# Mixer A of a two-layer encoder trunk: the left and right key tiles folded into one block before the softmax and put apart by GpSimd behind the transposes

## The chip, the cores and the metric

One core of one Trainium2 chip runs the whole program. The metric is the device time of one execution in microseconds (us), the median of three runs. Engine names as in the profile: PE is TensorE (matmuls and transposes), PEld its weight loads, DVE is VectorE, ACT is ScalarE, POOL is GpSimd, SP is SyncE, which mainly issues DMAs.

## The reference

Two layers over 1024 tokens (a grid of 16 rows by 64 columns) of width 1024 in fp32. Layer 0 uses mixer A, layer 1 mixer B; each is followed by a gated per-layer embedding, and one RMSNorm ends the trunk. Only mixer A is changed, and in it what the softmax of 16 heads of 64 works on:

```python
def mixer_a(h, w_in, rpb, w_out):
    proj = h @ w_in
    q, k, v, gate = jnp.split(proj, 4, axis=-1)          # 16 heads of 64
    ...                                                  # each query: a window of 8 rows x 16 columns of keys
    sc = jnp.einsum('bhqd,bhqnd->bhqn', qb, kg).astype(jnp.float32) * scale
    sc = sc + bb.astype(jnp.float32)[None]               # learned bias per offset
    pr = jax.nn.softmax(sc, axis=-1)
    o  = jnp.einsum('bhqn,bhqnd->bhqd', pr, vg)
    return (o * jax.nn.silu(gate)) @ w_out
```

A query at column c attends to the 16 columns from c - 8 on (clamped at the grid's edges).

## The kernel before, in words

Tokens are laid out in 8 tiles of 128: tile j holds the 8 grid columns 8j to 8j+7 of all 16 rows, so place p of a tile is row p // 8 and column p % 8 within the tile. With a window of 16 columns, the queries of tile j need keys of tiles j-1, j and j+1 alone: all of tile j, of tile j-1 the places whose column within the tile is at least the query's, and of tile j+1 those whose column is less. The mask `MK` says so with 1e30 in every other place, so for a query and a place of a tile, either the key in the left tile or the one in the right tile can count, never both.

Every fp32 product is made of fp32r pieces (a high part and the low rest), which is why most things exist twice: `PTh` and `PTl`, `HTh` and `HTl`, `wh` and `wl`. A head's q and k (transposed, 64 rows) are stacked to 128 rows: `QS` holds the high part of q in the lower 64 partitions and the low part in the upper, `KA` holds the high part of k twice, `KB` the low part of k twice.

**The attention steps.** `mixer_a` walks 128 steps (h, j): 16 heads of 8 query tiles. Step n issues, in this order, each as one item of a list:

- `f_T(n)`: transposes of the probabilities of step n by PE into the PSUM tile `t` (L723; two buffers), one for each key tile, so three for the inner tiles j = 1 to 6 and two for j = 0 and 7; ACT copies them as `PTh` (L726) and DVE subtracts the rest as `PTl` (L727). Both have 24 slots of 128 x 128: slot 3k + (j - k + 1) belongs to key tile k and query tile j, so that the up to three query tiles of one key tile lie side by side
- `f_E(n + 1)`: exponential on ACT over 384 columns (256 at j = 0 and 7), with the sum of each row (L715)
- `f_S(n + 2)`: scores of two steps ahead by PE into the PSUM tile `s` (two buffers), and on DVE, in one instruction, scores plus table `tb` and the minimum of each row, `mn` (L706; scores are negated, so that a minimum is the maximum)
- `f_AV(n - 2)`: PE multiplies v of key tile n - 2 with its slots of `PTh` and `PTl` into the PSUM tile `o`; it needs `f_T` up to step n - 1

**What runs beside.** `mix` puts pieces of dense work (the q/k projection of the next head, the gate, at the end p's projection) between the items, by a count of costs, and calls `pulse()` after each item of the steps: it loads and splits one weight tile when one is due (ACT `wh` L226, DVE `wl` L231), and counts down the list `post` of things to do a given number of pulses later. Among these are the splits of q and k, the evacuation of a head's output, and the tails of pairs of heads.

`qk_evac` copies q and k out of PSUM (ACT `th`, L647), and makes at pulses 2, 5 and 8 (`QD`): high q and high k on ACT (L650, L651); low q, low k and the second copy of high k on DVE (L654, L655, L656); the second copy of low k on DVE (L659).

`head_end` closes a head's half (four query tiles). For each pair of heads and half, two products follow on POOL, `Y*G` and `Y*rb` (L531, L532), where `rb` holds the reciprocal row sums and comes back from DRAM by DMA; they are issued at the head of a step, four steps after the half's last `f_AV`. Eleven pulses later ACT and DVE split Y (`rb<-Y` L528, L529). POOL also makes a head's table in five instructions (L681), and issues the DMAs that add up weights in DRAM (L597), one for each step in some heads.

Nothing is reordered at run time: each engine takes its instructions in the order in which the code issues them, and waits by semaphores.

Of the kernel before, what the change touches and what calls it, by code (L numbers as in the profile page):

```python
# [11 lines left out]
F32 = mybir.dt.float32  # L12
F32R = mybir.dt.float32r
# [28 lines left out]
THIRDS = {0: ((0, 1, 2), (0, 2, 1)), 1: ((0, 1, 2), (0, 1, 2))}  # L42
DP = 1
KD, KS = 3, 4
QD = (2, 5, 8)
QS_AT = 5
QO = (4, 6)
AGE, LAG = 3, 3
# [39 lines left out]
def lay_out(inp):  # L88
    g = {k: np.asarray(v) for k, v in inp.items()}
    W = np.empty((len(UNIT), 128, 1024), np.float32)  # L90

    def put(keys, cols, per):
        blk = cols.reshape(cols.shape[0] // 128, 128, -1).transpose(1, 0, 2)
        for u, key in enumerate(keys):
            W[UNIT[key]] = blk[:, u * per:(u + 1) * per].reshape(128, -1)

    aq, ak, av, ag = np.split(g["a_w_in"][0], 4, axis=1)
    for h in range(16):
        s = slice(h * HD, (h + 1) * HD)
        put([("aqk", h)], np.concatenate([aq[:, s], ak[:, s]], axis=1), 8)  # L100
    for q in range(4):
        put([("av", q, 0), ("av", q, 1)], av[:, q * 256:(q + 1) * 256], 4)
    bw = g["b_w_in"][0]
    bq, bk, bv, bg = bw[:, :1024], bw[:, 1024:1280], bw[:, 1280:1536], bw[:, 1536:]
    for p in range(8):
        s = slice(p * 128, (p + 1) * 128)
        put([("ag", p)], ag[:, s], 8)
        put([("bg", p)], bg[:, s], 8)
    for i in range(4):
        put([("bq", i, 0), ("bq", i, 1)], bq[:, i * 256:(i + 1) * 256], 4)  # L110
    for i in range(2):
# [24 lines left out]
    mask = np.where(ok, 0.0, BIG).astype(np.float32)  # L136

    inv = np.power(np.float32(10000.0), -np.arange(16, dtype=np.float32) * np.float32(2.0) / np.float32(32.0)).astype(np.float32)
    row = r.astype(np.float32)[:, None, None] + np.zeros((1, 8, 1), np.float32)
    col = (8 * np.arange(8)[None, :] + c[:, None]).astype(np.float32)[:, :, None]  # L140
    ar = (row * inv).astype(np.float32)
    ac = (col * inv).astype(np.float32)
    cosT = np.concatenate([np.cos(ar), np.cos(ar), np.cos(ac), np.cos(ac)], axis=2).astype(np.float32)
    sinT = np.concatenate([-np.sin(ar), np.sin(ar), -np.sin(ac), np.sin(ac)], axis=2).astype(np.float32)

    def swap(v):
        return v.reshape(2, 2, 16)[:, ::-1].reshape(64)

    bqn, bkn = g["b_q_norm"][0], g["b_k_norm"][0]
    hg = np.stack([bqn, swap(bqn), bkn, swap(bkn)])  # L150
    return {
        "x": tokens(g["x"][0]), "wts": W, "rpb": rpb, "gains": gains, "hgains": hg,
        "mask": mask, "rope": np.stack([cosT, sinT], axis=1),
        "gain0": gains[0].reshape(8, 128).T,
    }


@with_exitstack
def trunk(ctx, tc, x, wts, rpb, gains, hgains, mask, rope, gain0, out):
    nc = tc.nc  # L160
    sync, act, dve, pool, pe = nc.sync, nc.scalar, nc.vector, nc.gpsimd, nc.tensor

# [444 lines left out]
    def mixer_a():  # L607
        jobs = weight_sums()
        with ExitStack() as es:
# [4 lines left out]
            sb = es.enter_context(tc.tile_pool(name="asb", bufs=2))  # L614
            V = one.tile([128, NT, 4, 128], F32R, name="V")
            MK = one.tile([128, 5, 128], F32, name="MK")

            def dalloc():
                return pd.tile([128, 512], F32, name="d")
# [17 lines left out]
            def qk_evac(h, hf):  # L637
                def evac(ps):
                    if hf == 0:
                        QS[h] = qkp.tile([128, 1024], F32R, name="QS")  # L640
                        KA[h] = qkp.tile([128, 1024], F32R, name="KA")
                        KB[h] = qkp.tile([128, 1024], F32R, name="KB")
                    s = slice(hf * 512, (hf + 1) * 512)
                    lo, hi = slice(0, 64), slice(64, 128)
                    qs, ka, kb = QS[h], KA[h], KB[h]
                    raw = sb.tile([128, 512], F32, name="th", bufs=2)
                    act.activation(raw, ps, AF.Copy)  # L647

                    def one():
                        act.activation(qs[lo, s], raw[lo], AF.Copy, scale=-0.125)  # L650
                        act.activation(ka[hi, s], raw[hi], AF.Copy)  # L651

                    def two():
                        dve.scalar_tensor_tensor(qs[hi, s], raw[lo], -0.125, qs[lo, s], op0=ALU.mult, op1=ALU.subtract)  # L654
                        dve.tensor_tensor(kb[hi, s], raw[hi], ka[hi, s], ALU.subtract)  # L655
                        dve.tensor_copy(ka[lo, s], ka[hi, s])  # L656

                    def three():
                        dve.tensor_copy(kb[lo, s], kb[hi, s])  # L659
                    for i, f in enumerate((one, two, three)):  # L660
                        if h == 0:
                            f()
                        else:
                            post.add(QD[i], f)
                return evac

            def qk_items(h):
# [18 lines left out]
            def near(j):  # L686
                return max(j - 1, 0), min(j + 1, NT - 1)

            def f_S(h, j):
# [12 lines left out]
                else:  # L702
# [4 lines left out]
                                         in0=ps[:, :n].rearrange("p (k c) -> p k c", c=128), in1=tb,  # L707
                                         scale=1.0, scalar=1e38, op0=ALU.add, op1=ALU.min, accum_out=mn)
                SP[h, j] = (sp, mn)

            def f_E(h, j):
                k0, k1 = near(j)
                n = (k1 - k0 + 1) * 128
                sp, mn = SP[h, j]
                act.activation(sp[:, :n], sp[:, :n], AF.Exp, bias=mn, scale=-1.0, accum_out=RS[h][:, j:j + 1])  # L715

            def f_T(h, j):
                k0, k1 = near(j)
                m = k1 - k0 + 1
                sp, _ = SP.pop((h, j))  # L720
                ps = psT.tile([128, 4, 128], F32, name="t")
                for i in range(m):
                    pe.transpose(ps[:, i], sp[:, i * 128:(i + 1) * 128], ident)  # L723
                f0 = k0 * 3 + (j - k0 + 1)
                sl = slice(f0, f0 + 2 * m - 1, 2)
                act.activation(PTh[:, sl], ps[:, :m], AF.Copy)  # L726
                dve.tensor_tensor(PTl[:, sl], ps[:, :m], PTh[:, sl], ALU.subtract)  # L727

            def talloc():
                return psT.tile([128, 4, 128], F32, name="t")  # L730
# [122 lines left out]
            vs[1][1]()  # L853
            newton(4)
            sync.dma_start(MK, mask)
            for c in range(8):
                sync.dma_start(U[:, c], rpb[:, :, 7 - c:31 - c])
            for t in range(2, NT):
# [24 lines left out]
            psO = es.enter_context(tc.tile_pool(name="apo", bufs=2, space=PSUM))  # L883
            qkp = es.enter_context(tc.tile_pool(name="qkp", bufs=2))
            ptp = es.enter_context(tc.tile_pool(name="ptp", bufs=1))
            PTh = ptp.tile([128, NT * 3, 128], F32R, name="PTh")
            PTl = ptp.tile([128, NT * 3, 128], F32R, name="PTl")
            for d in qk_items(0):
                d[0]()
                WQ.pump()  # L890
# [12 lines left out]
            def av_and_v(h, kb):  # L903
                fs = [(lambda: f_AV(h, kb), CA[4])]
                if h % 4 == 3 and h < NH - 1:
                    fs += [(f, 0.0) for f in v_items(h // 4 + 1, kb)]
                return fs

            for h in range(NH):
                att = []  # L910
                for j in range(NT):
# [12 lines left out]
                        att.append((lambda n=n: f_E(*steps[n + 1]), CA[2]))  # L924
                    if n + 2 < len(steps):
                        att.append((lambda n=n: f_S(*steps[n + 2]), CA[3]))
                    if n >= 2:
                        att += av_and_v(*steps[n - 2])
                    if h == 15 and j >= YLOAD_A:
                        for t in ((j - YLOAD_A,) if j < NT - 1 else range(j - YLOAD_A, NT)):  # L930
                            att.append((lambda t=t: load_y(0, t), 0.0))
                    if h == 14 and j == OPEN3:
                        att.append((open3, 0.0))
                if h == NH - 1:
                    att += [(lambda: f_AV(NH - 1, NT - 2), CA[4]), (lambda: f_AV(NH - 1, NT - 1), CA[4])]
                dense = []
                if h < NH - 1:
                    dense += qk_items(h + 1)
# [754 lines left out]
    dense_phase(1)  # L1693


NAMES = ["x", "wts", "rpb", "gains", "hgains", "mask", "rope", "gain0"]


# [13 lines left out]
```

## Time and profile before

| what | value |
|---|---|
| median of three runs | 1531.36 us (1530.58 to 1531.82) |
| profiled execution, its own time | 1530.75 us |
| its span (first to last instruction) | 1529.0 us |
| PE, PEld busy | 1499.0 us (98%), 1312.1 us (86%) |
| DVE, ACT, POOL busy | 1099.1 us (72%), 899.6 us (59%), 305.0 us (20%) |
| mean granted TensorE clock | 0.999 |
| attention of mixer A | from about 60 us to about 522 us of the span |

The attention steps begin with the first transposes of probabilities at 60 us and end with the last ones at 522 us; a head takes about 24.5 us, and every fourth head about 42 us, since v of the next four heads is projected there. Matmuls overlap in the array, so PE counts as busy nearly throughout; what a matmul costs is read from the distance of starts, and what PE waits for from the idle time noted in a group's row. Durations of POOL are rough.

### The profile page before, as it was taken

How to read it: one execution, taken by the hardware profiler on the slowest of the kernel's cores; microseconds unless marked ns; L12 is line 12 of the kernel's file. 1: busy time of each engine (PE TensorE's matmuls, PEld its weight loads, DVE VectorE, ACT ScalarE, POOL GpSimd, SP SyncE). 2: the span in 40 equal slices, each digit the busy share in tenths (PEclk: the TensorE clock that was granted, in tenths of full speed). 3: DMA queues.
4: the chain of work that ended last, by engine and by line, in shares of the span. 5: the costliest groups of instructions: out<-in, count | busy, mean ns of one | idle time of the engine just before them, and what ended most of it. 6: DMA issues, size and time to landing. Idle time of an engine off the chain costs nothing.

```text
span 1529.0 us, 24364 instructions
## 1 busy us (share of the span) xinstructions
PE 1499.0 (98%) x8976; PEld 1312.1 (86%) x8976; DVE 1099.1 (72%) x2091; ACT 899.6 (59%) x1801; POOL 305.0 (20%) x413
## 2 busy tenths in 40 slices
PE   9999999999999999999999999999999999999997
PEld 8888988988988887888988889989899888778786
DVE  7666576477477499767877786777877777689856
ACT  6565465466366635433567776666767777744432
POOL 1222232242112000010312132443131300000022
PEclk9999999999999999999999999999999999999999
DMA  8325355262122863262210111111111122663123
GB/s 261 129 85 135 83 142 162 63 169 80 36 87 73 327 247 97 90 203 79 75 49 22 32 40 49 46 32 51 49 32 43 45 69 81 226 224 114 67 88 134
DMA packets 91096, 157.22 MB, mean 103 GB/s; under 512 B 18144, under 2 KB 54112, under 8 KB 90464
## 3 DMA queue, kind: packets, MB, share of 16 engines
q1 hardware_dynamic: 85824, 139.66, 27.4%
q0 software_dynamic: 2560, 8.39, 3.1%
q10 hardware_dynamic: 2592, 7.61, 1.4%
q8 instruction: 71, 1.16, 0.3%
q14 instruction: 49, 0.40, 0.1%
HBM read 125.10 MB, written 50.83 MB: 115 GB/s over the span
## 4 chain that ended last, share of the span: by engine, by line
PE 36%; DVE 10%; ACT 4%; issue 3%; DMA 0%; SPq 0%; ACTq 0%; DVEq 0%
PE d L317 17%; PE o L317 7%; PE t L1178 5%; PE s L317 5%; DVE PTl L1181 2%; DVE mn L1162 1%; ACT P L1168 1%; ACT PTh L1180 1%; PE t L317 1%; DVE xn L1498 1%; DVE QS L1142 0%; DVE wl L231 0%; DVE X L1394 0%; PE t L1132 0%; ACT wh L226 0%
## 5 line engine op out<-in xcount | busy, mean ns | idle before, releaser
L317 PE MATMUL d<-wh,HTh 128*128 128x256 f32 (+1 forms) x1032 | 343.0, 334 | 3.6 <-ACT HTh L446 0.8
L317 PE MATMUL d<-wh,HTl 128*128 128x256 f32 (+1 forms) x1032 | 337.9, 329 | 0.3 <-DVE HTl L447 0.3
L317 PE MATMUL d<-wl,HTh 128*128 128x256 f32 (+1 forms) x1032 | 337.2, 329 | 0.0
L1181 DVE TENSOR_TENSOR PTl<-t,PTh 128x512 fp32r<-128x512 f32 x256 | 164.4, 684 | 111.6 <-ACT PTh L1180 111.2
L317 PEld LDWEIGHTS d<-wh,HTh 128*128 128x128 f32 x1032 | 194.6, 189 | 24.3 <-ACT HTh L446 1.2
L317 PEld LDWEIGHTS d<-wl,HTh 128*128 128x128 f32 x1032 | 194.8, 190 | 18.9
L317 PEld LDWEIGHTS d<-wh,HTl 128*128 128x128 f32 x1032 | 194.7, 190 | 18.7 <-DVE HTl L447 0.5
L317 PE MATMUL d<-HTh,wh 128*128 128x512 f32 x504 | 206.0, 409 | 0.0
L317 PE MATMUL d<-HTh,wl 128*128 128x512 f32 x504 | 198.4, 394 | 0.0
L317 PE MATMUL d<-HTl,wh 128*128 128x512 f32 x504 | 197.6, 392 | 0.0
L1168 ACT ACTIVATE P<-s,mn 128x1024 f32<-128x1024 f32 x128 | 142.7, 1115 | 59.7 <-DVE mn L1162 59.0
L1180 ACT ACTIVATE PTh<-t 128x512 fp32r<-128x512 f32 x256 | 140.0, 593 | 44.6 <-PE t L1178 44.3
L1162 DVE TENSOR_REDUCE mn<-s 128x1 f32<-128x1024 f32 x128 | 154.8, 1210 | 12.3 <-PE s L317 12.2
L1178 PE MATMUL t<-ident,P 128*128 128x128 f32 x1024 | 137.6, 275 | 6.1 <-DVE PTl L1181 4.0
L317 PE MATMUL s<-KA,QS 128*128 128x512 f32 (+2 forms) x384 | 133.8, 402 | 0.0
L1178 PEld LDWEIGHTS t<-ident,P 128*128 128x128 f32 x1024 | 114.6, 140 | 21.9 <-DVE PTl L1181 15.9
L231 DVE TENSOR_TENSOR wl<-wstage,wh 128x1024 fp32r<-128x1024 f32 x78 | 101.0, 1300 | 35.6 <-ACT wh L226 35.1
L317 PE MATMUL s<-KB,QS 128*128 128x512 f32 (+2 forms) x384 | 121.8, 371 | 0.0
L727 DVE TENSOR_TENSOR PTl<-t,PTh 128x384 fp32r<-128x384 f32 (+1 forms) x128 | 66.6, 521 | 74.5 <-ACT PTh L726 73.3
L317 PE MATMUL o<-PTh,V 128*128 128x256 f32 (+2 forms) x672 | 118.9, 288 | 1.2 <-DVE Y L461 0.9
L317 PE MATMUL o<-PTl,V 128*128 128x256 f32 (+2 forms) x672 | 119.1, 288 | 0.1
L317 PEld LDWEIGHTS d<-HTh,wl 128*128 128x128 f32 x504 | 94.7, 188 | 21.5
(237 smaller groups left out, 2698.5 us busy)
## 6 DMA issues: line engine op xcount, KB each, us to landing
wstage<-in_wts SPq DMA_DIRECT2D x88, 512.0 KB
pp<-ppD SPq DMA_DIRECT2D x32, 256.0 KB
X<-in_x SPq DMA_DIRECT2D x15, 512.0 KB
rb<-rD SPq DMA_DIRECT2D x56, 128.0 KB
ppD<-th SPq DMA_DIRECT2D x20, 256.0 KB
tD0t<-in_wts SPq DMA_DIRECT2D x16, 256.0 KB
tD1t<-in_wts SPq DMA_DIRECT2D x16, 256.0 KB
xD<-X SPq DMA_DIRECT2D x8, 512.0 KB
```

The costliest lines, as they stand in the source:

```text
L231: eng.tensor_tensor(lo[:, c:c + n], s[:, c:c + n], hi[:, c:c + n], ALU.subtract)
L317: pe.matmul(ps, a, b, start=first, stop=last, skip_group_check=True)
L727: dve.tensor_tensor(PTl[:, sl], ps[:, :m], PTh[:, sl], ALU.subtract)
L1162: dve.tensor_reduce(mn, ps, axis=AX.X, op=ALU.min)
L1168: act.activation(p, ps, AF.Exp, bias=mn, scale=-1.0, accum_out=RS[h, hf][:, t:t + 1])
L1178: pe.transpose(ps[:, i], p[:, k * 128:(k + 1) * 128], ident)
L1180: act.activation(PTh[:, ks, c], ps, AF.Copy)
L1181: dve.tensor_tensor(PTl[:, ks, c], ps, PTh[:, ks, c], ALU.subtract)
L1498: dve.scalar_tensor_tensor(xn, X[t], rn[m][:, i:i + 1], g1, op0=ALU.mult, op1=ALU.mult)
```

## The change

The score instruction still covers three tiles and its row minimum. Then, for inner query tiles, a second DVE instruction writes the minimum of the left and the right block over the left one (128 x 128). The exponential covers 256 columns instead of 384, and two blocks are transposed instead of three. The middle one goes to its slot; the folded one goes to one of two new slots behind the 24 (by j's parity), and POOL multiplies it with the two 0/1 patterns of `SIDE` (key column not less than the query's; less) into the two slots of the left and the right key tile, once for `PTh` and once for `PTl`. `f_AV` runs three steps behind instead of two. `SIDE` is loaded once, behind `MK`. Apart from that, the second copies of high and low k move from DVE to ACT, and the five parts of the q/k split come at pulses 2, 4, 6, 7 and 9.

```diff
-QD = (2, 5, 8)
+QD = (2, 4, 6, 7, 9)
...
+    sides = np.stack([c[:, None] >= c[None, :], c[:, None] < c[None, :]], axis=1).astype(np.float32)
...
-                    def two():
+                    def low_q():
                         dve.scalar_tensor_tensor(qs[hi, s], raw[lo], -0.125, qs[lo, s], op0=ALU.mult, op1=ALU.subtract)
+
+                    def low_k():
                         dve.tensor_tensor(kb[hi, s], raw[hi], ka[hi, s], ALU.subtract)
-                        dve.tensor_copy(ka[lo, s], ka[hi, s])
-
-                    def three():
-                        dve.tensor_copy(kb[lo, s], kb[hi, s])
-                    for i, f in enumerate((one, two, three)):
+
+                    def across(k):
+                        act.activation(k[lo, s], k[hi, s], AF.Copy)
+                    parts = (one, low_q, lambda: across(ka), low_k, lambda: across(kb))
+                    for at, f in zip(QD, parts):
...
                 SP[h, j] = (sp, mn)
+                if 0 < j < NT - 1:
+                    dve.tensor_tensor(sp[:, 0:128], sp[:, 0:128], sp[:, 256:384], ALU.min)
 
             def f_E(h, j):
-                k0, k1 = near(j)
-                n = (k1 - k0 + 1) * 128
+                n = 256
...
             def f_T(h, j):
...
+                inner = 0 < j < NT - 1
+                for i in range(2):
+                    c = 1 - i if inner else i
+                    pe.transpose(ps[:, i], sp[:, c * 128:(c + 1) * 128], ident)
+                k0 = near(j)[0]
+                f0 = 3 * j + 1 if inner else k0 * 3 + (j - k0 + 1)
+                f1 = 3 * NT + j % 2 if inner else f0 + 2
+                sl = slice(f0, f1 + 1, f1 - f0)
+                act.activation(PTh[:, sl], ps[:, :2], AF.Copy)
+                dve.tensor_tensor(PTl[:, sl], ps[:, :2], PTh[:, sl], ALU.subtract)
+                if inner:
+                    def apart():
+                        for pt in (PTh, PTl):
+                            pool.tensor_tensor(pt[:, 3 * j - 1:3 * j + 4:4], pt[:, f1:f1 + 1].to_broadcast([128, 2, 128]), SIDE,
+                                               ALU.mult)
+                    apart()
...
+            sync.dma_start(SIDE, sides)
...
-            PTh = ptp.tile([128, NT * 3, 128], F32R, name="PTh")
-            PTl = ptp.tile([128, NT * 3, 128], F32R, name="PTl")
+            PTh = ptp.tile([128, NT * 3 + 2, 128], F32R, name="PTh")
+            PTl = ptp.tile([128, NT * 3 + 2, 128], F32R, name="PTl")
...
-                    if n >= 2:
-                        att += av_and_v(*steps[n - 2])
+                    if n >= 3:
+                        att += av_and_v(*steps[n - 3])
```

PE, in a head with no work on v, from one inner step's transposes to the next product with v, before (`t` the transposes, `d` dense work, `s` the scores, `o` the product with v):

```order
L723 MATMUL t<-ident,sp 128x128 x3
L317 MATMUL d<-HTh,wh_2073 128x512
L317 MATMUL d<-HTl,wh_2073 128x512
L317 MATMUL d<-HTh,wl_2074 128x512
L317 MATMUL d<-HTh,wh_2073 128x512
L317 MATMUL d<-HTl,wh_2073 128x512
L317 MATMUL d<-HTh,wl_2074 128x512
L317 MATMUL s<-KA,QS 128x384
L317 MATMUL s<-KB,QS 128x384
L317 MATMUL o<-PTh,V 128x384
L317 MATMUL o<-PTl,V 128x384
```

The same place on PE after the change:

```order
L728 MATMUL t<-ident,sp 128x128 x2
L318 MATMUL d<-HTh,wh_2165 128x512
L318 MATMUL d<-HTl,wh_2165 128x512
L318 MATMUL d<-HTh,wl_2166 128x512
L318 MATMUL d<-HTh,wh_2165 128x512
L318 MATMUL d<-HTl,wh_2165 128x512
L318 MATMUL d<-HTh,wl_2166 128x512
L318 MATMUL s<-KA,QS 128x384
L318 MATMUL s<-KB,QS 128x384
L318 MATMUL o<-PTh,V 128x256
L318 MATMUL o<-PTl,V 128x256
```

One transpose of the inner step is gone, and the product with v at the same place belongs to a key tile one step older (here the head's first key tile, which has two query tiles and so 256 columns, where the second with its three stood); the rest of PE's order stands.

POOL in head 6, with the tables of heads 7 and 8 around it, before (`tb` a head's table, `Y` the two products of a half, twice):

```order
L681 TENSOR_TENSOR tb<-MK,u 128x128 x5
L531 TENSOR_TENSOR Y<-Y,G 128x512
L532 TENSOR_TENSOR Y<-Y,rb 128x512
L531 TENSOR_TENSOR Y<-Y,G 128x512
L532 TENSOR_TENSOR Y<-Y,rb 128x512
L681 TENSOR_TENSOR tb<-MK,u 128x128 x5
```

After, from the products of step (6, 2) to those of step (6, 3):

```order
L738 TENSOR_TENSOR PTh<-PTh,SIDE 128x2x128
L738 TENSOR_TENSOR PTl<-PTl,SIDE 128x2x128
L532 TENSOR_TENSOR Y<-Y,G 128x512
L533 TENSOR_TENSOR Y<-Y,rb 128x512
L738 TENSOR_TENSOR PTh<-PTh,SIDE 128x2x128
L738 TENSOR_TENSOR PTl<-PTl,SIDE 128x2x128
```

Each inner step now has two products on POOL, and the Y products of a half, which come one step later than before, stand between them.

ACT in head 6 from step 3 to step 5 before (`sp` an exponential, `th`, `QS`, `KA` the q/k split, `wh` a weight's split, `rb<-Y` the split of Y):

```order
L726 ACTIVATE PTh<-t 128x3x128
L715 ACTIVATE sp,rs<-sp,mn 128x384
L528 ACTIVATE rb<-Y 128x512
L726 ACTIVATE PTh<-t 128x3x128
L715 ACTIVATE sp,rs<-sp,mn 128x384
L647 ACTIVATE th<-d 128x512
L226 ACTIVATE wh_2727<-wstage 128x1024
L650 ACTIVATE QS<-th 64x512
L651 ACTIVATE KA<-th 64x512
L726 ACTIVATE PTh<-t 128x3x128
L715 ACTIVATE sp,rs<-sp,mn 128x384
```

After:

```order
L733 ACTIVATE PTh<-t 128x2x128
L662 ACTIVATE KA<-KA 64x512
L720 ACTIVATE sp,rs<-sp,mn 128x256
L662 ACTIVATE KB<-KB 64x512
L733 ACTIVATE PTh<-t 128x2x128
L720 ACTIVATE sp,rs<-sp,mn 128x256
L649 ACTIVATE th<-d 128x512
L227 ACTIVATE wh_2805<-wstage 128x1024
L529 ACTIVATE rb<-Y 128x512
L652 ACTIVATE QS<-th 64x512
L653 ACTIVATE KA<-th 64x512
L733 ACTIVATE PTh<-t 128x2x128
```

The two copies of k are new on ACT, and the split of Y, whose half ends one step later, now stands in the run of q/k and weight work ahead of step 5's `PTh`.

More of the change, by code (lines that the diff above doesn't have):

```diff
@@ L152, in lay_out @@
         "x": tokens(g["x"][0]), "wts": W, "rpb": rpb, "gains": gains, "hgains": hg,
-        "mask": mask, "rope": np.stack([cosT, sinT], axis=1),
+        "mask": mask, "sides": sides, "rope": np.stack([cosT, sinT], axis=1),
         "gain0": gains[0].reshape(8, 128).T,
@@ L158, in trunk @@
 @with_exitstack
-def trunk(ctx, tc, x, wts, rpb, gains, hgains, mask, rope, gain0, out):
+def trunk(ctx, tc, x, wts, rpb, gains, hgains, mask, sides, rope, gain0, out):
     nc = tc.nc
@@ L616, in mixer_a @@
             MK = one.tile([128, 5, 128], F32, name="MK")
+            SIDE = one.tile([128, 2, 128], F32, name="SIDE")
             def dalloc():
@@ L663, in evac @@
                         else:
-                            post.add(QD[i], f)
+                            post.add(at, f)
                 return evac
@@ L717, in f_T @@
             def f_T(h, j):
-                k0, k1 = near(j)
-                m = k1 - k0 + 1
                 sp, _ = SP.pop((h, j))
                 ps = psT.tile([128, 4, 128], F32, name="t")
[L722 to L727, printed above, removed]
+                inner = 0 < j < NT - 1
[14 more added lines that the diff above has]
+                    apart()
             def talloc():
@@ L934, in mixer_a @@
                 if h == NH - 1:
-                    att += [(lambda: f_AV(NH - 1, NT - 2), CA[4]), (lambda: f_AV(NH - 1, NT - 1), CA[4])]
+                    att += [(lambda k=k: f_AV(NH - 1, k), CA[4]) for k in range(NT - 3, NT)]
                 dense = []
@@ L1693, in trunk @@
     dense_phase(1)
-NAMES = ["x", "wts", "rpb", "gains", "hgains", "mask", "rope", "gain0"]
+NAMES = ["x", "wts", "rpb", "gains", "hgains", "mask", "sides", "rope", "gain0"]
 def kernel(**inputs):
```

## The prediction

> **What bounds the kernel now.** I read the page's busy times first, then the stretch of mixer A's attention by itself, then the groups by shape, and last the timeline at the places that the change touches. The page, with its span and its engines:
>
> ```profile
> span 1529.0 us, 24364 instructions
> PE 1499.0 (98%) x8976; PEld 1312.1 (86%) x8976; DVE 1099.1 (72%) x2091; ACT 899.6 (59%) x1801; POOL 305.0 (20%) x413
> ```
>
> The windows view, from the first transposes of probabilities to the last (start and end, length, then busy time of PE, PEld, DVE, ACT and POOL, clock, DMA share, GB/s), and the groups view for these transposes:
>
> ```profile
> 60.00:522.00 462.00, 460.42 (x2646) 402.96 (x2645) 291.31 (x657) 271.54 (x610) 106.17 (x130) 1.00 0.40 116
> ```
>
> ```profile
> L723 PE MATMUL t<-ident,sp 128*128 128x128 f32 x352 | 60.2, 275 | 1.4 <-ACT sp L715 1.0
> ```
>
> PE is busy 460.4 of 462.0 us, at full clock, and waited 1.4 us in all ahead of the 352 transposes. So the stage is PE's, and whatever leaves PE's queue there comes off the time as long as nothing else makes PE wait. DVE has 171 us of room, ACT 190, POOL 356.
>
> **Part 1: 96 transposes less on PE.** A busy time of 275 ns says little, since matmuls overlap; the timeline merges transposes that follow each other, in sets of four, three and two:
>
> ```profile
> 701.30 0.60 PE L445 MATMUL t<-ident,xn 128*128 128x128 f32 x4
> ```
>
> ```profile
> 232.20 0.49 PE L723 MATMUL t<-ident,sp 128*128 128x128 f32 x3
> ```
>
> ```profile
> 522.03 0.38 PE L723 MATMUL t<-ident,sp 128*128 128x128 f32 x2
> ```
>
> Each one more adds 0.11 us. The change takes one from each of 6 x 16 inner steps: 96 x 0.11 = 10.6 us off PE, which is on the path. The bounds are zero, if a weight load behind it paces PE anyway, and 0.275 each, 26.4 in all.
>
> The Trainium skill, "TensorE: Matmul & The Clock Gate", Part 4: PE-mode transpose, puts one 128 x 128 transpose at about 275 ns inside a kernel. The row's mean duration agrees (275), the starts 0.11 us apart do not; by that figure 26.4 us would go, which is a rival below.
>
> **Part 2: ACT and DVE.** Groups by shape, inner steps first, then those that have two tiles already:
>
> ```profile
> L715 ACT ACTIVATE sp<-sp,mn 128x384 f32<-128x384 f32 x96 | 58.9, 614 | 8.1 <-DVE mn L706 7.5
> L715 ACT ACTIVATE sp<-sp,mn 128x256 f32<-128x256 f32 x32 | 16.2, 505 | 6.4 <-DVE mn L706 6.4
> L726 ACT ACTIVATE PTh<-t 128x384 fp32r<-128x384 f32 x96 | 47.1, 490 | 56.3 <-PE t L723 55.5 <-PE d L317 0.3
> L726 ACT ACTIVATE PTh<-t 128x256 fp32r<-128x256 f32 x32 | 12.2, 383 | 10.6 <-PE t L723 10.3
> L727 DVE TENSOR_TENSOR PTl<-t,PTh 128x384 fp32r<-128x384 f32 x96 | 53.4, 557 | 64.2 <-ACT PTh L726 63.3
> L727 DVE TENSOR_TENSOR PTl<-t,PTh 128x256 fp32r<-128x256 f32 x32 | 13.2, 413 | 10.3 <-ACT PTh L726 10.0
> L651 ACT ACTIVATE KA<-th 64x512 fp32r<-64x512 f32 x32 | 20.1, 629 | 0.6
> L656 DVE CAST KA<-KA 64x512 fp32r<-64x512 f32 x32 | 15.2, 476 | 1.0
> L997 DVE TENSOR_TENSOR qt<-th,tab 128x128 f32<-128x128 f32 x8 | 2.5, 311 | 0.0
> ```
>
> ACT: 96 x (614 - 505 + 490 - 383) ns = 20.7 us less, 64 copies of k at 0.63 = 40.3 more, so 272 becomes 291 us. DVE: 96 x 0.144 = 13.8 less, 64 copies at about 0.46 = 29 less, 96 minima at 0.31 = 30 more, so 291 becomes 279. Neither fills the 451 us that are left; both lie beside PE, unless their turn comes late (part 4).
>
> **Part 3: 192 products on POOL.** No row has this shape with these operands. The nearest are two-operand products of 128 x 256, in mixer B and in the start:
>
> ```profile
> L997 POOL TENSOR_TENSOR qt<-qt,tab 128x256 f32<-128x256 f32 x24 | 18.7, 777 | 1.9
> L231 POOL TENSOR_TENSOR wl<-wstage,wh 128x256 fp32r<-128x256 f32 x12 | 9.5, 820 | 29.1 <-ACT wh L226 29.1
> L436 POOL TENSOR_SCALAR xn<-X,stn 128x512 f32<-128x512 f32 x6 | 11.9, 1991 | 23.2 <-DVE stn L336 19.4 <-issue 3.8
> ```
>
> I take 0.76 (the first two less some waiting), with 1.0 (half of the third) as the upper end: 146 us, so POOL goes from 106 to 252 of 451. Two steps of head 6, and DMAs that POOL issues:
>
> ```profile
> 234.50 0.49 PE L723 MATMUL t<-ident,sp 128*128 128x128 f32 x3
> ```
>
> ```profile
> 195.42 3.40 POOL L597 DMA_DIRECT2D tD0t<-tD0t  x4
> ```
>
> The products of step n must be done when ACT and DVE refill the same extra slot, two steps on, and when PE multiplies key tile n - 1, at the end of step n + 2. A step takes 2.3 us (232.20 to 234.50) or 3.8 (240.70 to 244.54, below), so some 6 us are there for 1.5 us of work: hidden, as long as POOL isn't held up. Behind a late product stand the next step's products, Y's or a table on POOL; ACT's `PTh` of two steps on waits for it, and with it the exponential behind.
>
> POOL is held up by DVE, and DVE by POOL:
>
> ```profile
> 234.76 1.30 POOL L531 TENSOR_TENSOR Y<-Y,G 128x512 f32<-128x512 f32 x1 [1.84 <-DVE Y L461]
> ```
>
> ```profile
> 235.43 1.17 DVE L654 SCALAR_TENSOR_TENSOR QS<-th,QS 64x512 fp32r<-64x512 f32 x1
> 244.76 0.69 DVE L654 SCALAR_TENSOR_TENSOR QS<-th,QS 64x512 fp32r<-64x512 f32 x1
> 514.57 1.23 DVE L231 TENSOR_TENSOR wl<-wstage,wh 128x1024 fp32r<-128x1024 f32 x1 [2.60 <-ACT wh L226]
> 231.63 1.29 POOL L532 TENSOR_TENSOR Y<-Y,rb 128x512 f32<-128x512 f32 x1 [5.24 <-DMA rb<-rD]
> ```
>
> The DVE instruction, 0.69 us when alone (244.76), took 1.17 and ended 0.54 us after POOL's product did. `PTl` and the scores, which read PSUM, show no such stretch.
>
> The Trainium skill, "SBUF — State Buffer", section "SBUF: two separate sides", says that an instruction of DVE with two SBUF inputs and one of GpSimd that reads SBUF exclude each other for their whole length. The trace agrees (1.17 against 0.69). The rule speaks against this change: the new minimum has two SBUF inputs.
>
> **Part 4: where PE's turn comes.** The tight steps are 5 and 6 of a head. First DVE and ACT ahead of the transposes of step 5 (240.70), then ACT ahead of those of step 6 (244.54), in head 6:
>
> ```profile
> 238.28 0.55 DVE L706 CUSTOM_DVE_ANT_0 sp<-s,tb 128x384 f32<-128x384 f32 x1
> 239.19 0.61 ACT L715 ACTIVATE sp<-sp,mn 128x384 f32<-128x384 f32 x1
> 240.70 0.49 PE L723 MATMUL t<-ident,sp 128*128 128x128 f32 x3
> 240.54 0.60 ACT L647 ACTIVATE th<-d 128x512 f32<-128x512 f32 x1 [0.65 <-PE d L317]
> 241.04 1.05 ACT L226 ACTIVATE wh<-wstage 128x1024 fp32r<-128x1024 f32 x1
> 241.99 0.61 ACT L650 ACTIVATE QS<-th 64x512 fp32r<-64x512 f32 x1
> 242.61 0.63 ACT L651 ACTIVATE KA<-th 64x512 fp32r<-64x512 f32 x1
> 243.26 0.49 ACT L726 ACTIVATE PTh<-t 128x384 fp32r<-128x384 f32 x1
> 243.78 0.62 ACT L715 ACTIVATE sp<-sp,mn 128x384 f32<-128x384 f32 x1
> 244.31 0.19 ACT L715 ACTIVATION_READ_ACCUMULATOR sp<-sp,mn 128x1 f32 x1
> 244.54 0.55 PE L723 MATMUL t<-ident,sp 128*128 128x128 f32 x3
> ```
>
> Step 6: the exponential ends 244.50, PE starts 244.54, with no room. The change shortens ACT's run by 0.22 us and PE's way from step 5 by 0.11, and in six heads (2, 4, ... 12: those that follow a finished pair) it moves the split of Y (0.62 us) into this run. PE then waits 0.62 - 0.22 + 0.11 - 0.04 = 0.47 us in each: 2.8 us.
>
> Step 5: the scores' DVE instruction ends 238.83, the exponential could wait until about 239.9. In the same heads POOL now does Y's two products (1.3 each) just there, so low q waits behind the first, low k and the minimum behind the second or a new product. Laying the rows in the new order by hand, the minimum ends near 240.1 and PE waits 0.4; by how the turns fall it is 0 to 0.8. I take 0.3 x 6 = 1.8 us. In the other ten heads POOL has no Y products, and DVE no such wait; there I see none.
>
> Later POOL has no further deadline missed in that overlay: the products of step 6 end near 252.5, while PE needs them about 253. In heads 4 and 8, where DMAs that add up weights (three to four of 3.40 / 4 = 0.85 us) also stand between, I add 0.2 us each. Loading `SIDE` (0.13 MB at the start) and the later `f_AV` at the end of mixer A cost nothing that I can see: I leave 0 to 0.5 us for them.
>
> **Sum.** -10.6 + 2.8 + 1.8 + 0.4 = -5.6 us. The profiled execution took 1530.75 us, its span 1529.0; so 1525.15, and as the median of the runs lies 0.61 above that execution, **1525.8 us**.
>
> **Rivals.**
>
> *Nothing waits* (the turns of step 5 and 6 are covered): -10.6 and the 1.4 us of PE's waits too, so 1519 to 1522. For it: one overlay, and 190 us of room on ACT. Against: the 0.04 us at step 6.
>
> *The waits eat the gain*: 1.0 us at step 5 in all those heads and some in others, 1527 to 1533. For it: DVE takes its instructions in order, and a delay of low q passes on to `PTl`, the scores and the minimum.
>
> *Slower: POOL and DVE exclude each other throughout.* Between the products of step 2 and PE's turn at the products of step 6 there are 18.7 us in a head of that kind:
>
> ```profile
> 232.89 0.49 ACT L726 ACTIVATE PTh<-t 128x384 fp32r<-128x384 f32 x1
> ```
>
> ```profile
> 252.64 0.34 PE L317 MATMUL o<-PTh,V 128*128 128x384 f32 x1
> ```
>
> POOL has 10 x 0.76 + 4 x 1.3 = 12.8 us of work there; DVE's with two SBUF inputs are four of q and k at 0.69, two weights at 1.23 (the row at 514.57), three of Y and gate at 0.69, five minima at 0.31: 8.8. One after the other they are 21.6, 2.9 us late in each of seven heads: 20.3 - 10.6 = 10 us slower, 1541. At 1.0 us a product it is 1558. It turns the sign once over 84% of DVE's 8.8 us stand in POOL's way (1.5 us late a head). By the rule cited in part 3 (the Trainium skill, "SBUF — State Buffer") this is what comes of it if every turn collides. Against it: POOL has 5.9 us to spare in that stretch, and a DVE instruction that meets it idle costs nothing.
>
> *It does nothing to PE* (the third transpose hid under the next weight load): 1531. Against: 0.38, 0.49, 0.60.
>
> *A transpose is worth its 0.275 us*: 1530.75 - 26.4 + 0.6 = 1505. The starts speak against it.
>
> **Chances.** Forecast (1523 to 1528) 0.43; nothing waits 0.18; gain eaten 0.15, of which a third below 1528.3; slower 0.21, spread from 1534.5 to the 1558 above, with 1541 as its middle; no effect 0.02; the full duration 0.01. A measurement of this kernel tells 0.2% (3.1 us) from no change: faster means under 1528.3, slower over 1534.4. Faster: 0.43 + 0.18 + 0.05 + 0.01 = 0.67, less 0.03 for the forecast's own edge, 0.64; same 0.15; slower 0.21. Range 1519.5 to 1538: it takes in the first three cases and the near end of the slower one, some 0.05 of it, and leaves out 0.18.
>
> **What would show it.** Right: transposes in sets of two with starts 0.11 us apart; PE idle ahead of them in steps 5 and 6 of heads 2 to 12, some 0.5 us each, released by ACT's exponential; POOL's products at 0.7 to 0.9 us. Wrong: PE idle ahead of `o` for POOL (then the lock decides), idle time in heads without Y products, or no idle time at all; and a product over 1.2 us.

## The result, and the profile after

The changed kernel took 1541.18 us (median of 4 runs, 1538.39 to 1542.35) against 1531.49 us before: ratio 1.0062, 95% interval 1.0050 to 1.0074. It is slower by 10 us, where 1525.8 was forecast with a range of 1519.5 to 1538. The profiled execution took 1541.95 us. Its page, and the windows view of mixer A's attention, from the first transposes to the last (columns as before):

```profile
span 1540.2 us, 24589 instructions
PE 1493.7 (97%) x8880; PEld 1301.8 (85%) x8880; DVE 1118.4 (73%) x2123; ACT 921.0 (60%) x1865; POOL 449.6 (29%) x605
```

```profile
62.40:532.20 469.80, 455.18 (x2548) 392.17 (x2546) 312.32 (x690) 290.49 (x669) 250.66 (x322) 1.00 0.41 114
```

PE has 96 instructions less and is busy 5.3 us less over the whole execution, yet the stage is 469.8 us long instead of 462: PE now stands idle 14.6 us in it, where it was 1.6 before. It also begins 2.3 us later (62.43 against 60.16). Most of that is PE's clock: the first rounding of weights starts 2.0 us later (8.13 against 6.11 us), and from 12 to 16 us the mean granted clock is 0.57 (before: 1.00), which is 4.0 x 0.43 = 1.7 us. What PE waited for in the stage (us in all, times, longest), before and after:

```profile
PE t L723 <- ACT sp L715: 1.0, 2, 0.8
```

```profile
PE t L728 <- ACT sp L720: 13.5, 23, 2.0
PE d L318 <- ACT th L573: 1.0, 1, 1.0
```

Nothing waits for POOL. PE waits for ACT's exponential, 23 times instead of twice. The longest wait, in PE's timeline at the first two steps of head 5:

```profile
204.65 0.38 PE L728 MATMUL t<-ident,sp 128*128 128x128 f32 x2
...
209.09 0.44 PE L728 MATMUL t<-ident,sp 128*128 128x128 f32 x2 [1.96 <-ACT sp L720]
```

The set of two still shows its 0.38 us, so a transpose less is worth its 0.11. The wait stands at step 1 of a head in which POOL multiplies no Y. ACT's timeline ahead of it says why:

```profile
203.30 0.63 ACT L545 ACTIVATE th<-G 128x512 f32<-128x512 f32 x1
207.55 0.59 ACT L498 ACTIVATE Y<-o 64x512 f32<-64x512 f32 x1 [3.62 <-DMA yD0l<-Y]
208.17 0.38 ACT L733 ACTIVATE PTh<-t 128x256 fp32r<-128x256 f32 x1
208.45 0.50 ACT L720 ACTIVATE sp<-sp,mn 128x256 f32<-128x256 f32 x1
```

ACT stood 3.62 us at the merge of `o` into a new `Y`, until the DMA that stores an older `Y` had left that buffer; behind it in ACT's order stood `PTh` and the exponential for which PE waited. SP's timeline, before and after, shows that store:

```profile
187.26 1.30 SPq L468 DMA_DIRECT2D rD<-r8T  x4
190.51 1.09 SPq L470 DMA_DIRECT2D rb<-rD  x2
192.33 0.45 SPq L524 DMA_DIRECT2D yD0l<-Y  x1
```

```profile
193.27 1.33 SPq L469 DMA_DIRECT2D rD<-r8T  x4
198.53 1.09 SPq L471 DMA_DIRECT2D rb<-rD  x2
201.25 0.50 SPq L525 DMA_DIRECT2D yD0l<-Y  x1
```

Before, ACT's merge came at 197.90, 5.6 us behind the issue of the store, and waited for PE's product but not for the store:

```profile
197.90 0.59 ACT L497 ACTIVATE Y<-o 64x512 f32<-64x512 f32 x1 [0.82 <-PE o L317]
```

After, the store is issued 8.9 us later, of which 2.2 to 3.0 are the lateness of the head's own steps 4 to 7 (by the starts of their transposes), and the merge was due at 203.9, as soon as ACT had done `th`. The sums' trip through memory ahead of it (`rD`, `rb`) is 6 to 8 us later. All this hangs on the last product with V of a half head, and the change puts these products a step further behind.

By the starts of PE's instructions, waits of over 0.25 us ahead of transposes, summed by place (the kernel before has only 1.6 us in head 0 and 0.3 at step 3 in each of heads 4, 8 and 12):

| place | us |
|---|---|
| step 1 of heads 3, 5, 7, 9 (Y's store) | 4.6 |
| steps 5 and 6 of heads 2, 6, 10 | 2.6 |
| steps 4, 5, 6 of heads 4, 8, 12 | 5.7 |
| head 0 | 3.3 |
| head 15 (with a dense product that waits for `th`) | 2.6 |

Together these are 18.8 us, 16.3 more than before. With 1.7 us of slow clock behind the longest wait (last section) and 10.6 less for the transposes the stage should grow by 7.4 us; from the first transposes to the last it grew by 7.7 (469.6 against 461.9).

### The profile page after: what moved, and what is told of

Same layout as the page of the kernel before. It is cut to its first block, busy times and chain, and to the rows that moved or that the text cites. A ratio compares the mean times of both kernels' runs of the same rounds, so it can differ in the third digit from the quotient of the medians.

```text
span 1540.2 us, 24589 instructions
## 1 busy us (share of the span) xinstructions
PE 1493.7 (97%) x8880; PEld 1301.8 (85%) x8880; DVE 1118.4 (73%) x2123; ACT 921.0 (60%) x1865; POOL 449.6 (29%) x605
## 4 chain that ended last, share of the span: by engine, by line
PE 38%; DVE 9%; ACT 4%; issue 2%; DVEq 0%; ACTq 0%
PE d L318 18%; PE o L318 7%; PE t L1192 6%; PE s L318 6%; DVE PTl L1195 2%; DVE mn L1176 1%; ACT P L1182 1%; ACT PTh L1194 1%; PE t L318 1%; DVE xn L1512 1%; PE t L1146 0%; DVE X L1408 0%; DVE QS L1156 0%; DVE wl L232 0%; ACT wh L227 0%
## 5 line engine op out<-in xcount | busy, mean ns | idle before, releaser
L738 POOL TENSOR_TENSOR PTh<-PTh,SIDE 128x256 fp32r<-128x256 f32 x96 | 76.5, 797 | 210.7 <-ACT PTh L733 210.7
```

Source lines behind the costliest of these rows:

```text
L738: pool.tensor_tensor(pt[:, 3 * j - 1:3 * j + 4:4], pt[:, f1:f1 + 1].to_broadcast([128, 2, 128]), SIDE, ALU.mult)
```

## Experiments

The expectations name three theories. M, the merge chain: the later products with V delay everything behind a head's end, up to Y's store. L, the lock: POOL's products hold DVE, as the prediction's slower rival has it. K: ACT's copies of k stand in front of the exponential. Each ratio is against the kernel before on the same chip, with its 95% interval.

**Only the third step of lag** (`b_lag3`), in the kernel before:

```
-                    if n >= 2:
-                        att += av_and_v(*steps[n - 2])
+                    if n >= 3:
+                        att += av_and_v(*steps[n - 3])
...
+                    att += [(lambda k=k: f_AV(NH - 1, k), CA[4]) for k in range(NT - 3, NT)]
```

> The kernel before with one edit: each head's products with V come three steps behind the scores' transposes instead of two, nothing else. Theory M (the merge chain): a step later means that the last products of a head, the reciprocal of its sums, their trip through memory, Y's two products and Y's store all come some 5 us later, so that ACT's next merge of o waits until Y's store has landed (heads 3, 5, 7, 9), Y's split stands in ACT's queue ahead of the exponential of step 6, and the end of the mixer gets a key tile more. Without the new products POOL does Y's a little earlier than in the changed kernel, so I expect about half of the 11 us that these places cost there: 1537 (1534 to 1541). Theory L (the lock of POOL and DVE, the prediction's slower rival): there are no new products and no minimum, so 1531 to 1533.

1542.89 us, 1.0085 (1.0070 to 1.0100). One loop bound (with the end of the last head that belongs to it), without fold, minimum, products or copies, costs 11 us, as much as the whole change. PE's waits in the stage:

```profile
PE t L723 <- ACT sp L715: 9.8, 14, 1.5
```

M is right on the direction and too low on the size, and its half with the store is wrong here: Y's store in head 4 is issued at 198.50, 6.2 us later than before (in the changed kernel 8.9), and PE waits over 0.25 us for such a store only once (0.6 us, head 7). The rest is Y's split ahead of the exponential of step 6 in six heads (0.6 to 0.7 each), step 5 of heads 4, 8, 12 (1.05 each), heads 0 and 15 (1.2 and 2.0 more than before). Heads 4, 8 and 12 have another cause to consider: `av_and_v` issues the pieces of v's projection behind the products, so the bound moves these too, and the last piece now stands in step 2 of these heads instead of step 1. Ahead of their step 5 the exponential waits for DVE's scores, which stand behind two splits of weights (here in head 4):

```profile
192.80 0.61 ACT L715 ACTIVATE sp<-sp,mn 128x384 f32<-128x384 f32 x1 [1.69 <-DVE mn L706]
```

How much of these 3.2 us belongs to v's projection and how much to the head's end is not shown by any run.

The split of Y at step 6, in ACT's timeline of head 2 and PE's:

```profile
121.25 0.62 ACT L528 ACTIVATE rb<-Y 128x512 fp32r<-128x512 f32 x1
121.77 0.62 ACT L650 ACTIVATE QS<-th 64x512 fp32r<-64x512 f32 x1
122.40 0.63 ACT L651 ACTIVATE KA<-th 64x512 fp32r<-64x512 f32 x1
123.06 0.49 ACT L726 ACTIVATE PTh<-t 128x384 fp32r<-128x384 f32 x1
123.57 0.61 ACT L715 ACTIVATE sp<-sp,mn 128x384 f32<-128x384 f32 x1
```

```profile
124.33 0.44 PE L723 MATMUL t<-ident,sp 128*128 128x128 f32 x2 [0.53 <-ACT sp L715]
```

**The change with two steps of lag** (`a_lag2`: the two edits above undone in the changed kernel):

> The changed kernel with the products with V two steps behind again. M: the waits of heads 3, 5, 7, 9 (5.5 us with the slow matmuls behind the longest), the split at step 6 (3.0) and the longer end (3.1) go, 1541.2 - 11.6 = 1529.6, and PE now waits at o for POOL wherever POOL is late: with 0 to 6 us of that, 1530 to 1536. L: POOL has a step less for the same products, so 1541 or more, with PE idle ahead of o.

1539.68 us, 1.0056 (1.0043 to 1.0068): above M's 1530 to 1536 and below L's 1541. Both sides got a part: the exponential's waits halve, and PE waits for POOL at `o` instead, 7.6 us:

```profile
PE t L728 <- ACT sp L720: 6.9, 6, 1.9
PE o L318 <- POOL PTl L738: 4.3, 7, 0.9
PE o L318 <- POOL PTh L738: 3.3, 3, 1.4
```

So the third step does what it is there for. It costs as much as it saves.

**The products left out** (`a_noprod` at three steps of lag, `a_lag2_noprod` at two):

```
-                if inner:
+                if inner and h == 0:
                     def apart():
```

> The changed kernel with POOL's 192 products done in head 0 alone (left out: the putting apart of the folded blocks in heads 1 to 15, so that part of the probabilities is missing); folds, copies and the order of the rest stay. L: DVE isn't held any more, the late exponentials go: 1526 to 1529. M: Y's products come some 1.5 us earlier, which takes some 4 us from the waits for Y's store, the split and the end stay: 1535 to 1538.

> The changed kernel with V's products two steps behind, as before, and POOL's 192 products done in head 0 alone (left out: the putting apart in heads 1 to 15). What is left of the change is the fold, its shorter exponentials and copies, 96 transposes less, and the copies of k on ACT. If a transpose is worth its 0.11 us and neither minimum nor k copies make PE wait: 1531.5 - 10.5 + 0 to 3 = 1521 to 1524. If the k copies or the minimum cost PE something of their own: 1525 to 1530.

With three steps 1535.52, 1.0025 (1.0014 to 1.0036): of the 12 to 15 us that L expects only 5.7 come back, as M expects. With two 1523.80, 0.9956 (0.9944 to 0.9969). With the kernels above this makes a square:

| | two steps | three steps |
|---|---|---|
| without products | 1523.80 | 1535.52 |
| with products | 1539.68 | 1541.18 |

Fold, minimum and copies alone gain 7 us. Then either POOL's products (15.9) or the third step (11.7) takes more than that away, and both together little more than the first alone (17.4).

**A third buffer for Y**, in the changed kernel with and without its products (`a_ybuf`, `a_ybuf_noprod`):

```
-            Y = sb.tile([128, 512], F32, name="Y", bufs=2)
+            Y = sb.tile([128, 512], F32, name="Y", bufs=3 if layer == 0 else 2)
```

> The changed kernel with a third buffer for Y in mixer A, nothing else. M (ACT's merge of o in heads 3, 5, 7, 9 waits until the store of the pair before has left its Y): the four waits of 1.8 to 3.6 us on ACT go, and with them PE's 0.31 + 2.13 + 0.68 + 1.47 us and some 0.9 us of slowly granted clock behind the longest: 1541.2 - 5.5 = 1536. L (the lock of POOL and DVE makes these exponentials late): 1540 to 1542.

> The changed kernel with a third buffer for Y and POOL's 192 products in head 0 alone (left out: the putting apart in heads 1 to 15). What the products still cost, once Y's store stands in nobody's way, is the lock of POOL and DVE by itself. L: it is most of the 5.7 us that leaving them out gave with two buffers: 1528. M: the 5.7 us came through Y's store, and 0 to 1.5 are left: 1532 to 1534.

1533.61, 1.0017 (1.0008 to 1.0026), where M expected 1536, and without products 1533.07, 1.0015 (1.0007 to 1.0024). Two KB a partition take 7.6 us off the changed kernel. ACT's waits for the store are gone, and PE's are

```profile
PE t L728 <- ACT sp L720: 9.3, 19, 1.2
```

Once nobody waits for Y's store, leaving out 180 of the 192 products is worth 0.5 us, which is zero within the two intervals (some 2 us), and PE's waits for the exponential stay (9.6 us without the products). What the products cost in the changed kernel, they cost through the store, to which they are one more delay on POOL. So L is refuted as the cause there. What part of the 15.9 us at two steps is the lock, and what part POOL's own lateness, is not separated by these runs.

**Copies of k**, back on DVE in the changed kernel (`a_kdve`), and put on ACT in the kernel before (`b_kact`):

```
-QD = (2, 4, 6, 7, 9)
+QD = (2, 5, 8)
...
-                        act.activation(k[lo, s], k[hi, s], AF.Copy)
+                        dve.tensor_copy(ka[lo, s], ka[hi, s])
```

> The changed kernel with the copies of k back on DVE, in the three turns of before. Theory K (ACT's copy of the low half waits in ACT's queue for DVE's subtraction, with PTh and the exponential behind it, and the copy of the high half stands between two weight roundings in the heads after a V build): the waits at step 5 of heads 2, 6, 10 (0.36 each), at step 4 of heads 4, 8, 12 (0.64 each) and half of head 0's 1.8 us go: 1537. L: DVE has 29 us more in the same turns, held by POOL: 1543 or more. M alone: 1541.

> The kernel before with the repeating of k on ACT in the five turns of the changed kernel, and nothing else. Theory K (ACT's copy waits for DVE's subtraction with the exponential behind it): with the exponential's 0.04 us of room at step 6, waits of 0.3 to 0.6 us in most heads: 1534 to 1540. Rival (the move takes from DVE what makes its turns late, as the 12 us show that the changed kernel lost when the copies went back to DVE): 1529 to 1532.

1552.91, 1.0140 (1.0126 to 1.0154), and 1533.48, 1.0017 (1.0008 to 1.0025). K holds in small: 2.4 us in the kernel before, between its 1534 to 1540 and its rival's 1529 to 1532. In the changed one the move is no cost but saves 11.7, where K expected it to cost 4. DVE with minima and held operands has no turns left for the copies: ACT's exponentials wait 55.4 us for DVE with the copies there and 16.8 in the changed kernel, and PE waits 22.4 us for exponentials. Here L's expectation (1543 or more) was the better one. (In `a_kdve` the copy of high k comes ahead of low k, in the kernel before behind it.)

**Y's split behind step 6** (`a_ybuf_ys13`), on top of the third buffer:

```
-YS = (11, 11)
+YS = (13, 11)
```

> The changed kernel with a third buffer for Y, and Y's split two turns later, so that ACT does it behind the exponential of step 6 instead of ahead of it. If the prediction's step 6 holds (0.47 us in six heads, 0.50 in the trace), 3.0 us go from the 1533.6 of the third buffer alone: 1530.6 (1530 to 1532). Rival: the split then makes step 7 or 0 late, 1533 to 1535.

1543.91, 1.0078 (1.0064 to 1.0092): 10 us worse than the third buffer alone, and above both ranges that were expected. The waits at step 6 do go, and 1.9 us come at step 7 of the same six heads. The profiled execution is the slowest of the seven (1550.58): in it the clock falls behind five of its waits, which takes 8.5 us of PE's time (last section). DVE's, POOL's and PE's timelines in head 2:

```profile
125.41 0.88 DVE L530 TENSOR_TENSOR Y<-Y,rb 128x512 fp32r<-128x512 f32 x1 [0.66 <-ACT rb L529]
126.31 1.66 DVE L656 SCALAR_TENSOR_TENSOR QS<-th,QS 64x512 fp32r<-64x512 f32 x1
128.00 0.42 DVE L710 CUSTOM_DVE_ANT_1 sp<-s,tb 128x256 f32<-128x256 f32 x1
```

```profile
125.69 1.74 POOL L532 TENSOR_TENSOR Y<-Y,G 128x512 f32<-128x512 f32 x1
```

```profile
129.12 0.44 PE L728 MATMUL t<-ident,sp 128*128 128x128 f32 x2 [1.75 <-ACT sp L720]
```

DVE's half of the split, ahead of low q, pushes it into Y's product on POOL, and low q takes 1.66 us for the 0.69 of the prediction's row; the scores behind it are late by both. Here the lock does decide, through an old product and not a new one.

**Y's products two steps later** at two steps of lag (`a_lag2_fin6`: `FIN = (6, 4)`, three buffers for `Y` and `rb`):

> The changed kernel with V's products two steps behind, three buffers for Y and for the sums' rows, and Y's two products on POOL two steps later, so that POOL does not stand waiting for the sums' rows with the new products behind. If PE's waits at o (some 9 us in the even heads) come from that standing and from Y's products in the same stretch, most of them go and the time is 1526 to 1532; if POOL is late there for its work alone, 1536 to 1541.

1533.05, 1.0011 (1.0003 to 1.0020), 6.6 us less than with two steps alone; PE's wait for POOL falls from 7.6 to 1.6 us. Which of the two edits, the later products or the buffers, does it is not shown. The upper end of what was expected (1532) is missed by a little: 2.7 us stand at step 3 of head 15, whose cause is open.

**A larger mask** (`b_mask7`), in the kernel before:

```
+    mask = np.concatenate([mask, mask[:, :2]], axis=1)
```

> The kernel before with two unused blocks more in the mask (448 KB instead of 320 KB, one tensor and one transfer as before). All kernels with the sides so far, also the one that has them inside the mask, got their first weights 1.2 to 2.0 us later than those without (7.3 to 8.1 us against 6.1 to 6.4). If it is the place of the tensors in memory that the larger input moves, the first rounding of weights starts after 7.2 us here too and the time is 1532 to 1533.5; if it belongs to the fold's program, it starts at 6.1 to 6.4 and the time is 1530.5 to 1531.5.

1531.48, 1.0000 (0.9991 to 1.0009). ACT's first rounding of weights starts at 7.97 us, as late as in the kernels with the sides (8.13 after, 6.11 before), so the delay seems to come with the larger inputs and not with the fold. The stage starts 1.6 us later in this trace too (61.80), with the clock at 0.73 from 12 to 16 us. Yet the time stays below the 1532 to 1533.5 that was expected for this case: a cost of the delay is not to be told from zero within 1.4 us.

**The fold in odd heads alone** (`odd_fold`), with two steps of lag, the sides inside the mask, and ACT copying k only where an odd head runs beside it:

```
+                if h % 2 and 0 < j < NT - 1:
                     dve.tensor_tensor(sp[:, 0:128], sp[:, 0:128], sp[:, 256:384], ALU.min)
...
+                if h % 2 == 0:
...
+                    return
```

> The kernel before with the fold, POOL's products and the copies of k on ACT in the odd heads alone, where POOL has no products of Y; V's products two steps behind as before, and the two halves of the sides in the same tensor and transfer as the mask. M and the PE waits for POOL seen with two steps: the odd heads had no waits there, so half of the fold's 10.5 us stays and nothing is added: 1526 (1525 to 1529). If the start comes later for the added input tensor, that goes too; if not, 1 to 2 us more. L: POOL's products hold DVE in the odd heads as well, 1531 or more.

1526.00, 0.9969 (0.9957 to 0.9981): faster than both kernels, by about the 5.3 us that 48 transposes of 0.11 are worth. PE's wait for the exponential is what it was before the change, and the 0.7 us for `G` lie behind the last transposes, where the kernel before has them too:

```profile
PE t L741 <- ACT sp L732: 1.0, 2, 0.8
PE d L319 <- ACT G L574: 0.7, 1, 0.7
```

## Why the prediction was wrong, by its own steps

- **Transposes, -10.6:** right. Sets of two take 0.38, and with half of them `odd_fold` gains half.
- **POOL's products, 0.76 each:** 0.80 and 0.86 in the groups view below, and POOL's 250.7 us in the stage are the 252 that were forecast. Hidden behind PE, as said; no PE wait for POOL.

```profile
L738 POOL TENSOR_TENSOR PTl<-PTl,SIDE 128x256 fp32r<-128x256 f32 x95 | 81.5, 858 | 9.7 <-DVE PTl L734 9.7
L738 POOL TENSOR_TENSOR PTh<-PTh,SIDE 128x256 fp32r<-128x256 f32 x95 | 75.8, 798 | 208.5 <-ACT PTh L733 208.5
```

- **Step 6, 0.47 in six heads:** right: 0.50 to 0.52 in each (from the start of the matmul before; a row's bracket counts from its modelled end and is smaller), with the split of Y in front (247.96 in the rows below).
- **Step 5, 0.3 in six heads:** 0.36 in heads 2, 6, 10, but 0.58, 0.58 and 1.11 in heads 4, 8, 12. In heads 2, 6 and 10 the instruction that comes last is another than the prediction's. ACT, DVE, POOL and PE in head 6:

```profile
245.10 0.63 ACT L662 ACTIVATE KB<-KB 64x512 fp32r<-64x512 f32 x1 [1.96 <-DVE KB L659]
245.64 0.36 ACT L733 ACTIVATE PTh<-t 128x256 fp32r<-128x256 f32 x1
246.02 0.51 ACT L720 ACTIVATE sp<-sp,mn 128x256 f32<-128x256 f32 x1
...
247.96 0.62 ACT L529 ACTIVATE rb<-Y 128x512 fp32r<-128x512 f32 x1
...
250.18 0.51 ACT L720 ACTIVATE sp<-sp,mn 128x256 f32<-128x256 f32 x1
```

```profile
243.81 1.26 DVE L659 TENSOR_TENSOR KB<-th,KA 64x512 fp32r<-64x512 f32 x1
```

```profile
242.20 1.63 POOL L533 TENSOR_TENSOR Y<-Y,rb 128x512 f32<-128x512 f32 x1
```

```profile
246.68 0.44 PE L728 MATMUL t<-ident,sp 128*128 128x128 f32 x2 [0.19 <-ACT sp L720]
...
250.83 0.44 PE L728 MATMUL t<-ident,sp 128*128 128x128 f32 x2 [0.34 <-ACT sp L720]
```

ACT's new copy of k waits 1.96 us for DVE's low k, which POOL's product of Y held, and the exponential stands behind the copy. A wait on another engine had moved into ACT's order, and the prediction priced only ACT's time. In heads 4, 8 and 12 a copy between two weight roundings adds 0.64 at step 4, for which the sum had no term. At their step 5 ACT's exponential does wait for DVE's minimum, as the prediction has it (1.36 us in head 4), but `b_lag3` shows 1.05 us of PE's time at this place without any minimum.

- **The term that failed** is the one of "0 to 0.5 us" for the load of `SIDE` "and the later `f_AV` at the end of mixer A". It looked at the products with V as PE's work, moved by a step and costing nothing. But a head's end releases a chain: merge, reciprocal, a trip through memory by two DMAs, two products on POOL, split, store. That chain had been laid so that its pieces fell between the exponentials and its store was done when the buffer was needed. A step later, together with the pieces of v's projection, it costs 11 us by itself (`b_lag3`), and with the products of POOL in front of Y's it costs 7.6 us through one buffer (`a_ybuf`). Of all this the prediction had only the split at step 6. It forecast 1525.15 us for the profiled execution, which took 1541.95. Of these 16.8 us, 6.3 stand at Y's store with the slow clock behind it, 4.3 are more waiting in heads 0 and 15, 3.3 are more at steps 4 to 6 than was forecast, 2.3 lie ahead of the stage and 1.2 behind it (0.8 us of waits at step 3 went away). The other half of the term, the load, can't be told from zero in the time (`b_mask7`).
- **The slower rival gave 1541, and 1541 was measured, for another reason.** The agreement is chance. L's place was seven heads with Y's products and PE late at step 6; the longest waits are in heads without them, and the sign that the prediction names for the lock, PE idle ahead of `o` for POOL, is absent. Leaving out the products returns 5.7 us, or 0.5 with the third buffer.
- **The lock as a row** is real: the minimum takes 517 ns on average with the products and 391 without (groups view, changed kernel and `a_noprod`), and at the worst place 2.58 us, from 203.62 to 206.20, while POOL's two products ran from 204.05 to 205.74:

```profile
L715 DVE TENSOR_TENSOR sp<-sp 128x128 f32<-128x128 f32 x95 | 49.1, 517 | 3.3
```

```profile
L715 DVE TENSOR_TENSOR sp<-sp 128x128 f32<-128x128 f32 x94 | 36.7, 391 | 3.3
```

```profile
203.62 2.58 DVE L715 TENSOR_TENSOR sp<-sp 128x128 f32<-128x128 f32 x1
```

It was done at 206.20, and its exponential started at 208.45 for ACT's wait: hidden. DVE is busy 312.3 us in the stage, where the prediction's part 2 adds up to 279 from rows of the kernel before. These rows agree with the rule of the Trainium skill ("SBUF — State Buffer", section "SBUF: two separate sides") that the prediction cites. What the lock does to the time depends on whether DVE is the last to come.

Left open: why the third step costs 2.0 us in head 15 and 1.2 in head 0, and where the 1.2 us come from by which the part behind the stage grew.

## What to carry to other kernels

When a step of a software pipeline is moved, follow what its last instruction releases until the buffers are free again, not only the instruction itself: a chain of small steps on several engines and DMAs moves along, and a transfer that was in time comes late. More lag for a new helper engine can cost as much as the helper's lateness (here 11.7 and 15.9 us, and 17.4 with both); putting the helper only where it has room (here the odd heads) kept the old lag and half the gain. And a rival that gives the measured time is not yet the cause: its place and its signs have to be there too.

## What the runs showed of the hardware

The granted clock of PE fell after a wait of only 1.96 us. The windows view around head 5's (length, PE, PEld, DVE, ACT, POOL, then the clock):

```profile
206.00:209.00 3.00, 1.13 (x6) 0.67 (x4) 1.56 (x5) 1.43 (x4) 3.00 (x7) 1.00 1.09 260
209.00:211.00 2.00, 1.91 (x9) 1.60 (x10) 1.97 (x6) 0.42 (x2) 1.14 (x2) 0.89 1.00 187
211.00:214.00 3.00, 3.00 (x10) 2.63 (x9) 1.17 (x4) 0.60 (x2) 1.46 (x2) 0.51 0.54 115
214.00:217.00 3.00, 3.00 (x18) 2.62 (x17) 1.38 (x4) 2.37 (x6) 1.44 (x3) 1.00 0.33 61
```

It comes more than 1 us after PE is busy again and lasts about 3 us: 3.0 x 0.49 + 2.0 x 0.11 = 1.7 us of PE's time, nearly as much as the wait itself. The Trainium skill, "TensorE: Matmul & The Clock Gate", Part 1: The HAM clock gate, gives an idle window of some 3.4 us for the fall to half; here less sufficed.

The length of the wait alone does not decide it. In `a_ybuf_ys13` PE waits about 1.75 us at step 7 of six heads; the clock falls in four of them and stays at 1.00 in heads 2 and 10. The windows behind the wait in head 2 and in head 4:

```profile
129.00:133.00 4.00, 3.88 (x21) 3.32 (x22) 3.44 (x9) 3.28 (x8) 4.00 (x8) 1.00 1.11 391
203.00:207.00 4.00, 4.00 (x16) 3.46 (x17) 2.18 (x7) 3.11 (x7) 3.82 (x6) 0.63 0.99 301
```

In `a_kdve` a wait of 2.5 us at step 5 of head 4 is followed by a clock of 1.00 (202 to 206 us). What decides is not shown.
